# Four seams between layers in a fixed order: sums, norm and columns tile by tile

## The chip, the cores and the metric

The kernel runs on one core of a Trainium2 chip. The metric is the device time of one execution in microseconds (us). The core's engines run side by side, each through its own queue of instructions in order: PE (TensorE, matrix products), DVE (VectorE, elementwise work), ACT (ScalarE, activations and casts), POOL (GpSimd, elementwise work and some transfers) and SP (SyncE), whose queue issues most of the transfers from HBM. Three runs of the kernel before took 2445.11 to 2447.05 us, median 2446.44.

## The reference

Two blocks of two layers each run over 256 tokens of width 1024, in fp32. The first block's layers have a gated delta rule (gdn) and a windowed attention (dsw) as mixers, and a gated feed-forward network (ffn) of hidden size 2816. The second block's layers have an "even" and an "odd" attention over the tokens and a context, and a mixture of 16 experts (MoE). Around each mixer and each ffn or MoE stands the same frame, in which shift, scale and gate come from a conditioning vector through a matrix product (the "ada" work):

```python
def rms_norm(x, gain):
    xf = x.astype(jnp.float32)
    y = xf * lax.rsqrt(jnp.mean(xf * xf, axis=-1, keepdims=True) + RMS_EPS)
    return y * gain.astype(jnp.float32)
...
h_lat = modulate(rmsnorm(x, norm_mix[i]), m[:, :, 0], m[:, :, 1])   # h * (1 + scale) + shift
...
x = x + m[:, :, 2] * y_lat
h_lat = modulate(rmsnorm(x, norm_ffn[i]), m[:, :, 3], m[:, :, 4])
```

So between two layers every token's row of x is finished (x + gate · y), its root mean square is taken, and the scaled, modulated row is what the next matrix product reads. A place where this happens is called a seam here.

## The kernel before

The 256 tokens are two tiles of 128 rows, tile 0 and tile 1. x lies in SBUF with tokens on partitions. A matrix product wants its input with features on partitions, so each tile's 1024 features are turned into 8 blocks ("columns") of 128x128. Products are made in three passes (`mm3`, lines 394 to 398): every fp32 operand is split into a rounded part and the rest, hi and lo for the input, whi and wlo for the weights, and hi·whi, hi·wlo and lo·whi are added up. `split_w` makes whi with a cast on ACT (line 387) and wlo with a subtraction (line 391), which runs on DVE or, for some chunks, on POOL: every sixth in the first ffn, and in the second ffn (`ffn1`) the first four (`pool_next`).

The steps of a seam and their lines are these. The output product of the layer ends in PSUM; per tile and half (512 features) DVE multiplies by the gate (440) and adds to x (442). `norm_rows` squares each half on ACT with a running sum (299), adds the two sums (300), and takes the inverse root with Ln and Exp on ACT (157, 158) and a correction step in 128x1 operations on DVE (156, 159, 161, 162). DVE scales the tile's 1024 features (302). `split_T` transposes 8 blocks on PE (311) into PSUM, modulates them in four steps a chunk of 512, one chunk of a tile on DVE (329) and the other on ACT (326), and casts to hi on ACT (332) and lo on DVE (333). Then the next product's first matmuls can start (396 to 398).

The four seams are: 1, from the output product of gdn to ffn0, near 384 to 395 us; 2, from ffn0 to dsw, near 600 to 615; 3, from dsw to ffn1, near 891 to 906; 4, from ffn1 to the even attention, near 1099 to 1118.

Other work runs beside this chain. The ada products (218) take their weights as they come; the second block's context runs ahead during the first block, with a gather by one-hot products (1720) at seam 3, and its keys for the even attention are split with cast and subtraction (1309, 1310) at seam 4. `gate()` spreads a gate's row over all partitions before the even attention, with two products on POOL (284), four matmuls (288) and two copies on ACT. Line 1598 and 1601 prepare a router's weights.

The order of each engine's instructions is not written by hand: a planner that simulates the timeline places them, and may move any instruction ahead of another as long as data and buffers allow. Two means restrict it: `keep_in_program_order` sets an instruction behind the last one so marked on its engine, and `issue_after` sets it behind a named instruction.

## Time and profile before

| | |
|---|---|
| median of three runs | 2446.44 us (2445.11 to 2447.05) |
| profiled execution | 2443.09 us, its span 2441.3 us |
| mean granted PE clock | 0.941 |
| busy: PE, DVE, ACT, POOL | 87%, 45%, 32%, 13% |
| mean rate of the transfers | 278 GB/s |
| moved in all | 677.57 MB |

The span is what the profiler saw between the first and the last instruction; the time of an execution lies a little above it. Busy shares are averages over stages of different kinds. The first 1290 us are the first block and the even attention, where PE is busy nearly throughout, with short breaks; from then on the experts' weights stream in at up to 427 GB/s, with the odd attention (about 1830 to 1970) between the two mixtures. The granted clock of PE is 1.0 (2.4 GHz) or 0.5 (1.2 GHz) at any moment; a mean over a stretch says how much of each it had.

### The profile page before, as it was taken

The numbers are of one execution on the slowest core, as the hardware profiler recorded it, in microseconds if no ns is written. First come the engines' busy times: TensorE is split into PE (matmuls) and PEld (weight loads), VectorE is DVE, ScalarE is ACT, GpSimd is POOL, SyncE is SP. The second block draws the span as 40 slices with busy tenths as digits, with TensorE's granted clock in tenths as the row PEclk, the third lists the DMA queues.
The fourth block names the chain that finished last, engine by engine and source line by source line (L and its number), as shares of the span: only waits on it lengthen the run. The fifth ranks groups of instructions, "written<-read, shape, count | busy, mean of one in ns | idle before, by whom it ended". The sixth has DMA issues, their size and how long they took to land. (4 is left out here: it accounts for less than half of the span.)

```text
span 2441.3 us, 30277 instructions
## 1 busy us (share of the span) xinstructions
PE 2123.6 (87%) x12053; PEld 1278.1 (52%) x12053; DVE 1100.0 (45%) x2051; ACT 773.9 (32%) x1470; POOL 316.8 (13%) x334
## 2 busy tenths in 40 slices
PE   6987998998999979998988998888888987777777
PEld 3864676786677657885575222222265652222222
DVE  3777357866555575547764121212157731101111
ACT  3564344443555544435443100000047530000000
POOL 3344211112000040003411000000021010000000
PEclk8988998999999979999998999999989989989999
DMA  9657766976332356537746999999921469999998
GB/s 351 247 174 240 238 226 218 362 256 215 126 109 85 126 189 203 167 119 264 296 169 267 425 426 427 425 426 426 415 84 63 162 274 426 426 426 425 427 425 349
DMA packets 152445, 677.57 MB, mean 278 GB/s; under 512 B 15937, under 2 KB 38315, under 8 KB 113648
## 3 DMA queue, kind: packets, MB, share of 16 engines
q1 hardware_dynamic: 143072, 637.98, 67.3%
q0 software_dynamic: 6784, 36.48, 4.3%
q8 instruction: 95, 1.56, 0.3%
q10 hardware_dynamic: 2448, 1.18, 0.2%
q14 instruction: 46, 0.38, 0.0%
HBM read 667.07 MB, written 8.52 MB: 277 GB/s over the span
## 5 line engine op out<-in xcount | busy, mean ns | idle before, releaser
L391 DVE TENSOR_TENSOR wlo<-rawt,whi 128x1024 fp32r<-128x1024 f32 (+2 forms) x257 | 308.7, 1207 | 228.0 <-ACT whi L387 225.6
L387 ACT CAST whi<-rawt 128x1024 fp32r<-128x1024 f32 (+3 forms) x284 | 280.5, 995 | 313.7 <-PE mmt L398 118.9
L1872 PE MATMUL anyt<-rawb,xs 128*32 128x512 f32 x672 | 164.4, 650 | 52.0 <-DMA rawb<-in_w_exp_gate 26.7
L1858 PE MATMUL anyt<-rawb,xs 128*32 128x512 f32 x1472 | 175.2, 614 | 26.6 <-DMA rawb<-in_w_exp_up 17.3
L1832 DVE TENSOR_TENSOR y<-anyt,g 32x512 f32<-32x512 f32 (+1 forms) x120 | 66.4, 553 | 214.7 <-PE anyt L1825 206.9
L1825 PE MATMUL anyt<-rawb,hT 128*32 128x256 f32 (+1 forms) x1056 | 132.9, 491 | 21.2 <-DMA rawb<-in_w_exp_down 11.0
L398 PE MATMUL anyt<-whi,lo 128*128 128x512 f32 (+1 forms) x384 | 144.8, 379 | 1.8 <-DVE lo L333 1.8
L397 PE MATMUL anyt<-wlo,hi 128*128 128x512 f32 (+1 forms) x384 | 145.4, 380 | 1.1 <-DVE wlo L391 1.1
L1877 DVE TENSOR_TENSOR h<-anyt,h 64x512 f32<-64x512 f32 x16 | 11.1, 693 | 281.8 <-ACT h L1876 281.8
L396 PE MATMUL anyt<-whi,hi 128*128 128x512 f32 (+1 forms) x384 | 134.4, 381 | 0.4 <-ACT t L1723 0.4
L1876 ACT ACTIVATE h<-anyt 64x512 f32<-64x512 f32 x16 | 9.4, 589 | 392.4 <-PE anyt L1872 392.4
L1862 ACT ACTIVATE h<-anyt 128x512 f32<-128x512 f32 x16 | 9.6, 597 | 378.1 <-PE anyt L1858 378.1
L1872 PEld LDWEIGHTS anyt<-rawb,xs 128*32 128x32 f32 x672 | 39.3, 118 | 171.0 <-issue 100.7
L1858 PEld LDWEIGHTS anyt<-rawb,xs 128*32 128x32 f32 x1472 | 48.8, 112 | 147.1 <-issue 113.4
L1863 DVE TENSOR_TENSOR h<-anyt,h 128x512 f32<-128x512 f32 x16 | 11.1, 692 | 207.8 <-PE anyt L1858 207.8
L1825 PEld LDWEIGHTS anyt<-rawb,hT 128*32 128x32 f32 (+1 forms) x1056 | 49.5, 128 | 94.3 <-issue 65.0
L218 PE MATMUL adat<-rawt,lhs 128*32 128x512 f32 x448 | 73.6, 665 | 29.0 <-DMA rawt<-in_w_ada 24.9
L391 POOL TENSOR_TENSOR wlo<-rawt,whi 128x1024 fp32r<-128x1024 f32 (+1 forms) x27 | 67.6, 2511 | 237.7 <-ACT whi L387 196.2
L1872 PE MATMUL anyt<-rawt,xs 128*32 128x512 f32 x352 | 78.7, 596 | 10.9 <-DMA rawt<-in_w_exp_gate 7.3
L397 PEld LDWEIGHTS anyt<-wlo,hi 128*128 128x128 f32 x384 | 72.5, 189 | 20.5 <-issue 3.2
L398 PEld LDWEIGHTS anyt<-whi,lo 128*128 128x128 f32 x384 | 72.4, 188 | 16.2 <-DVE lo L333 2.2
L396 PEld LDWEIGHTS anyt<-whi,hi 128*128 128x128 f32 x384 | 71.6, 189 | 16.6 <-issue 0.8
(634 smaller groups left out, 4381.2 us busy)
## 6 DMA issues: line engine op xcount, KB each, us to landing
rawt<-in_w_ada SPq DMA_DIRECT2D x96, 1024.0 KB, 7.0
rawb<-in_w_exp_up SPq DMA_DIRECT2D x41, 2048.0 KB, 27.0
rawb<-in_w_exp_down SPq DMA_DIRECT2D x41, 2048.0 KB, 27.0
rawb<-in_w_exp_gate SPq DMA_DIRECT2D x39, 2048.0 KB, 25.6
rawt<-in_w_exp_gate SPq DMA_DIRECT2D x41, 1024.0 KB, 26.5
rawt<-in_w_ffn_in SPq DMA_DIRECT2D x40, 1024.0 KB, 7.7
rawt<-in_w_exp_up SPq DMA_DIRECT2D x38, 1024.0 KB, 27.0
rawt<-in_w_exp_down SPq DMA_DIRECT2D x31, 1024.0 KB, 27.0
```

Source lines behind the costliest of these rows:

```text
L218: nc.tensor.matmul(bank[32 * j:32 * j + 32, :], lhs[:, k, :], r[:, 0, 512 * j:512 * j + 512], start=(k == 0), stop=(k == 7))
L387: nc.scalar.copy(hi, w)
L391: e.tensor_tensor(out=lo, in0=w, in1=hi.bitcast(F32), op=OP.subtract)
L396: nc.tensor.matmul(ps, xh, wh, start=start, stop=False)
L397: nc.tensor.matmul(ps, xh, wl, start=False, stop=False)
L398: nc.tensor.matmul(ps, xl, wh, start=False, stop=stop)
L1825: nc.tensor.matmul(yb[o:o + M, c:c + n], hT[:, k, :], w[:, i * n:i * n + n], start=(k == 0), stop=(k == KT - 1), **({} if S == 2 else dict ...
L1832: nc.vector.tensor_tensor(out=ys[s][p0:p0 + CAP, 256 * q:256 * (q + n)], in0=yb[o:o + CAP, c:c + 256 * n], in1=g2[o:o + CAP, 256 * q:256 * ...
L1858: nc.tensor.matmul(b[CAP * i:CAP * i + CAP, :], lhs(k0 + j, i % 2), r[:, j, 512 * hf:512 * hf + 512], start=(k0 + j == 0), stop=(k0 + j == ...
L1863: nc.vector.tensor_tensor(out=h, in0=banks[1], in1=h, op=OP.mult)
L1872: nc.tensor.matmul(b[o:o + 32, :], lhs(k0 + j), r[:, j, 512 * hf:512 * hf + 512], start=(k0 + j == 0), stop=(k0 + j == KT - 1), tile_posit ...
L1877: nc.vector.tensor_tensor(out=h[0:64, :], in0=b[64:P, :], in1=h[64:P, :], op=OP.mult)
```

## The change

At the four seams `norm_opens` takes the place of `norm_T`; the context's norm keeps `norm_T`. The squares go into tiles of their own. Instead of scaling the tile and transposing it, DVE scales the identity (`dg`, 128x128) with the inverse roots, and PE multiplies each 128x128 block of x with it, which gives the scaled block transposed. The DVE steps are kept in program order: the modulation's factor A, tile 0's products and sums, tile 0's inverse root and `dg`; at seams 1 to 3 tile 1's last or all products and sums follow only then (`late`). Tile 1's inverse root is set behind tile 0's Exp. The first three splits of the new weights are set behind named steps: the first cast behind tile 0's Exp and its subtraction behind the sums, the next two behind tile 0's last hi and lo. The context's attention, its keys' splits and the router's weights are set behind hi and lo of the norm. `ffn1` gives no split to POOL. `gate()` is called behind the even attention's projections instead of ahead of them, and the first matmuls of the second block's second-layer ada stay in program order. Modulation stays in four steps a chunk.

The diff, without the lines that only pass new arguments or mark one more matmul:

```diff
@@ -153,13 +154,32 @@
-        nc.vector.tensor_scalar(out=v, in0=ss, scalar1=scale, scalar2=eps, op0=OP.mult, op1=OP.add)
-        nc.scalar.activation(out, ss, AF.Ln, scale=scale, bias=self.eps)
-        nc.scalar.activation(out, out, AF.Exp, scale=-0.5)
-        nc.vector.tensor_tensor(out=t, in0=out, in1=out, op=OP.mult)
+        self.keep(nc.vector.tensor_scalar(out=v, in0=ss, scalar1=scale, scalar2=eps, op0=OP.mult, op1=OP.add))
+        self.keep(nc.scalar.activation(out, ss, AF.Ln, scale=scale, bias=self.eps))
+        self.last_exp = self.keep(nc.scalar.activation(out, out, AF.Exp, scale=-0.5))
+        self.keep(nc.vector.tensor_tensor(out=t, in0=out, in1=out, op=OP.mult))
         sg = -1 if neg else 1
-        nc.vector.scalar_tensor_tensor(out=t, in0=t, scalar=-0.5 * sg, in1=v, op0=OP.mult, op1=OP.mult)
-        nc.vector.scalar_tensor_tensor(out=out, in0=t, scalar=1.5 * sg, in1=out, op0=OP.add, op1=OP.mult)
+        self.keep(nc.vector.scalar_tensor_tensor(out=t, in0=t, scalar=-0.5 * sg, in1=v, op0=OP.mult, op1=OP.mult))
+        self.keep(nc.vector.scalar_tensor_tensor(out=out, in0=t, scalar=1.5 * sg, in1=out, op0=OP.add, op1=OP.mult))
+
+    def keep(self, ins):
+        return self.tc.keep_in_program_order(ins) if self.pin else ins
+
+    @contextmanager
+    def pinned(self):
+
+        self.pin = True
+        yield
+        self.pin = False
+
+    @contextmanager
+    def after(self, *names):
+
+        with ExitStack() as es:
+            for n in names:
+                if n in self.behind:
+                    es.enter_context(self.tc.issue_after(self.behind[n].ins))
+            yield
@@ -215,8 +235,10 @@
-                    nc.tensor.matmul(bank[32 * j:32 * j + 32, :], lhs[:, k, :],
-                                     r[:, 0, 512 * j:512 * j + 512], start=(k == 0), stop=(k == 7))
+                    i = nc.tensor.matmul(bank[32 * j:32 * j + 32, :], lhs[:, k, :],
+                                         r[:, 0, 512 * j:512 * j + 512], start=(k == 0), stop=(k == 7))
+                    if held and k == 0:
+                        self.tc.keep_in_program_order(i)
@@ -291,23 +313,32 @@
-    def norm_rows(self, x, t, xn, rsqrt=None):
+    def inv_rms(self, x, t, sq, rsqrt=None):
...
-            nc.scalar.activation(xn[:, 512 * h:512 * h + 512], x[:, t, 512 * h:512 * h + 512], AF.Square, accum_out=s2[:, h:h + 1])
-        nc.vector.tensor_tensor(out=ss, in0=s2[:, 0:1], in1=s2[:, 1:2], op=OP.add)
+            nc.scalar.activation(sq(h), x[:, t, 512 * h:512 * h + 512], AF.Square, accum_out=s2[:, h:h + 1])
+        self.keep(nc.vector.tensor_tensor(out=ss, in0=s2[:, 0:1], in1=s2[:, 1:2], op=OP.add))
         (rsqrt or self.rsqrt_e)(rs, ss, 1, 1.0 / D, 1e-6)
+        return rs
+
+    def norm_rows(self, x, t, xn, rsqrt=None):
+
+        nc = self.nc
+        rs = self.inv_rms(x, t, lambda h: xn[:, 512 * h:512 * h + 512], rsqrt)
...
-    def split_T(self, src, nk, t, hi, lo, A=None, B=None):
+    def split_T(self, src, nk, t, hi, lo, A=None, B=None, diag=None):
...
+                if diag is not None:
+                    nc.tensor.matmul(tp[:, P * j:P * j + P], src[:, P * (k0 + j):P * (k0 + j) + P], diag, start=True, stop=True)
+                    continue
@@ -329,8 +360,8 @@
-                nc.scalar.copy(h, m)
-                nc.vector.tensor_tensor(out=l, in0=m, in1=h.bitcast(F32), op=OP.subtract)
+                ends = nc.scalar.copy(h, m), nc.vector.tensor_tensor(out=l, in0=m, in1=h.bitcast(F32), op=OP.subtract)
+        return ends if A is not None else None
@@ -343,6 +374,36 @@
+    def norm_opens(self, x, gain, sc, sh, hi, lo):
+
+        nc = self.nc
+        late, self.late = self.late, None
+        self.behind, self.nbehind = {}, 0
+        with self.tc.tile_pool(reuse_waits="tile", name="xn", bufs=2, side="right") as pool:
+            def inv(t):
+                rs = self.inv_rms(x, t, lambda h: pool.tile([P, 512], F32, name="xsq"))
+
+                dg = pool.tile([P, P], F32, name="dg")
+                last = self.keep(nc.vector.tensor_scalar(out=dg, in0=self.ident, scalar1=rs, scalar2=None, op0=OP.mult))
+                return dg, last
+
+            A = self.small(KT)
+            with self.pinned():
+                self.keep(nc.vector.scalar_tensor_tensor(out=A, in0=sc, scalar=1.0, in1=gain, op0=OP.add, op1=OP.mult))
+                dg, last = inv(0)
+                exp = self.last_exp
+                if late:
+                    last = late()
+            for t in range(2):
+                if t:
+                    with self.after("exp"):
+                        dg, _ = inv(t)
+                ends = self.split_T(x[:, t, :], KT, t, hi, lo, A, sh, dg)
+                if t == 0:
+                    self.behind = dict(exp=exp, add=last, hi0=ends[0], lo0=ends[1])
+                self.behind.update(hi=ends[0], lo=ends[1])
+                self.nbehind = 3
@@ -384,11 +445,14 @@
-        nc.scalar.copy(hi, w)
+        self.nbehind -= 1
+        with self.after(*("exp",) if self.nbehind == 2 else ("hi0",) if self.nbehind >= 0 else ()):
+            nc.scalar.copy(hi, w)
...
-        e.tensor_tensor(out=lo, in0=w, in1=hi.bitcast(F32), op=OP.subtract)
+        with self.after(*("add",) if self.nbehind == 2 else ("lo0",) if self.nbehind >= 0 else ()):
+            e.tensor_tensor(out=lo, in0=w, in1=hi.bitcast(F32), op=OP.subtract)
@@ -427,7 +491,14 @@
-                if not pairs:
+                if ends and ci == len(cols) - 1:
+                    f = lambda ci=ci, t=t, b=banks[i]: consumer(ci, t, b)
+                    if i == len(tiles) - 1:
+                        self.late = f
+                    else:
+                        with self.pinned():
+                            f()
+                elif not pairs:
@@ -437,16 +508,16 @@
-            nc.vector.tensor_tensor(out=tm, in0=ps, in1=g[:, 512 * ci:512 * ci + 512], op=OP.mult)
+            self.keep(nc.vector.tensor_tensor(out=tm, in0=ps, in1=g[:, 512 * ci:512 * ci + 512], op=OP.mult))
             xs = x[:, t, 512 * ci:512 * ci + 512]
-            nc.vector.tensor_tensor(out=xs, in0=xs, in1=tm, op=OP.add)
+            return self.keep(nc.vector.tensor_tensor(out=xs, in0=xs, in1=tm, op=OP.add))
...
-        self.pool_share, self.pool_next = dict(ffn0=(6, 0), ffn1=(self.NEVER, 4))[key]
+        self.pool_share, self.pool_next = dict(ffn0=(6, 0), ffn1=(self.NEVER, 0))[key]
@@ -501,8 +572,15 @@
-                for h in range(2):
-                    f(h, t, banks[t][h])
+                def sums(t=t):
+                    for h in range(2):
+                        last = f(h, t, banks[t][h])
+                    return last
+                if t and key == "ffn0":
+                    self.late = sums
+                else:
+                    with self.pinned():
+                        sums()
@@ -891,7 +970,7 @@
-                    with self.aside():
+                    with self.aside(), self.after("hi", "lo"):
@@ -1306,8 +1385,9 @@
-                nc.scalar.copy(kh, src)
-                nc.vector.tensor_tensor(out=kl, in0=src, in1=kh.bitcast(F32), op=OP.subtract)
+                with self.after("hi", "lo"):
+                    nc.scalar.copy(kh, src)
+                    nc.vector.tensor_tensor(out=kl, in0=src, in1=kh.bitcast(F32), op=OP.subtract)
@@ -1321,7 +1401,6 @@
-            gate()
@@ -1336,6 +1415,7 @@
+            gate()
@@ -1595,10 +1675,11 @@
-        nc.vector.scalar_tensor_tensor(out=A, in0=sc, scalar=1.0, in1=gain, op0=OP.add, op1=OP.mult)
         wa = rp.tile([P, 2, KT, E], F32, name=f"wa{tag}")
-        for i, m in enumerate((A, sh)):
-            nc.vector.tensor_tensor(out=wa[:, i], in0=w_router, in1=m.unsqueeze(2).to_broadcast([P, KT, E]), op=OP.mult)
+        with self.after("lo"):
+            nc.vector.scalar_tensor_tensor(out=A, in0=sc, scalar=1.0, in1=gain, op0=OP.add, op1=OP.mult)
+            for i, m in enumerate((A, sh)):
+                nc.vector.tensor_tensor(out=wa[:, i], in0=w_router, in1=m.unsqueeze(2).to_broadcast([P, KT, E]), op=OP.mult)
@@ -1958,7 +2039,7 @@
-                        self.norm_T(xc[s], gmix(l), m[:, s, 8:16], m[:, s, 0:8], hi, lo, (0, 1))
+                        self.norm_opens(xc[s], gmix(l), m[:, s, 8:16], m[:, s, 0:8], hi, lo)
@@ -2068,7 +2149,7 @@
-                self.norm_T(x, gmix(l), m[:, 8:16], m[:, 0:8], hi, lo, (0, 1))
+                self.norm_opens(x, gmix(l), m[:, 8:16], m[:, 0:8], hi, lo)
@@ -2079,7 +2160,7 @@
-            self.norm_T(x, gffn(l), m[:, 32:40], m[:, 24:32], hi2, lo2, (0, 1))
+            self.norm_opens(x, gffn(l), m[:, 32:40], m[:, 24:32], hi2, lo2)
```

What the planner makes of it is shown at three places. A name like x<-x,t_5016 reads: written tile, then read tiles.

The first is DVE at seam 2, where ffn0's output becomes x and the norm for dsw begins. Before (the four products L440 stand a few rows above, in a row; modc is the modulation, va the norms' gains, smt small scratch):

```order
L442 TENSOR_TENSOR x<-x,t_5016 128x512
L442 TENSOR_TENSOR x<-x,t_5019 128x512
L442 TENSOR_TENSOR x<-x,t_5040 128x512
L442 TENSOR_TENSOR x<-x,t_5043 128x512
L1601 TENSOR_TENSOR wa_7269<-wr,A_7267 128x128
L338 SCALAR_TENSOR_TENSOR smt<-modc_118,va 128x8
L391 TENSOR_TENSOR wlo<-rawt,whi 128x1024
L300 TENSOR_TENSOR smt<-smt 128x1
L156 TENSOR_SCALAR smt<-smt 128x1
L159 TENSOR_TENSOR smt<-smt 128x1
```

and after, at the same place (the line numbers are those of the changed kernel; gb is the gate; 511 and 513 are 440 and 442, 393 is 338, 322 is 300, 157 is 156, 160 is 159):

```order
L511 TENSOR_TENSOR t_5020<-mmt,gb_120 128x512
L513 TENSOR_TENSOR x<-x,t_5020 128x512
L511 TENSOR_TENSOR t_5023<-mmt,gb_120 128x512
L272 COPY modc_118<-tpt 128x4x4
L393 SCALAR_TENSOR_TENSOR smt<-modc_118,va 128x8
L513 TENSOR_TENSOR x<-x,t_5023 128x512
L322 TENSOR_TENSOR smt<-smt 128x1
L157 TENSOR_SCALAR smt<-smt 128x1
L160 TENSOR_TENSOR smt<-smt 128x1
L162 SCALAR_TENSOR_TENSOR smt<-smt 128x1
L163 SCALAR_TENSOR_TENSOR smt<-smt 128x1
L388 TENSOR_SCALAR dg<-cst,smt 128x128
```

Tile 0's two halves are finished first and its diagonal is made at once; the weight's split and tile 1's products and sums, which stood ahead, now stand behind.

The second is POOL at seam 3, ahead of ffn1 (gr and gt are tables for the even attention). Before:

```order
L1300 TENSOR_SCALAR gr<-gr 128x2x64
L986 COPY gr<-gr 128x8x16 x2
L391 TENSOR_TENSOR wlo<-rawt,whi 128x1024 x3
L1304 TENSOR_TENSOR gt<-gr,ro 128x256 x4
L391 TENSOR_TENSOR wlo<-rawt,whi 128x1024
```

and after:

```order
L1379 TENSOR_SCALAR gr<-gr 128x2x64
L1065 COPY gr<-gr 128x8x16 x2
L1383 TENSOR_TENSOR gt<-gr,ro 128x256 x4
L219 MEMSET brow 128x512
L221 DMA brow<-in_b_ada 4x512
```

The four splits of weights are gone from POOL; they stand on DVE.

The third is PE at seam 4, where ffn1's last matmul (hl) is followed by the even attention's projections (h2i, h2l). Before:

```order
L398 MATMUL mmt<-whi,hl 128x512
L218 MATMUL adat<-rawt,lhs_108 32x512 x8
L288 MATMUL mmt<-t_9138,cst 128x512
L288 MATMUL mmt<-t_9143,cst 128x512
L218 MATMUL adat<-rawt,lhs_108 32x512 x4
L311 MATMUL tpt<-cst,xn 128x128 x8
L218 MATMUL adat<-rawt,lhs_108 32x512 x4
L311 MATMUL tpt<-cst,xn 128x128 x8
L396 MATMUL mmt<-whi,h2i_9148 128x512
```

and after (340 is the product with the diagonal, 238 is 218, 460 to 462 are 396 to 398):

```order
L462 MATMUL mmt<-whi,hl 128x512
L340 MATMUL tpt<-dg,x 128x128 x12
L460 MATMUL mmt<-whi,h2i_9150 128x512
L461 MATMUL mmt<-wlo,h2i_9150 128x512
L462 MATMUL mmt<-whi,h2l_9151 128x512
L460 MATMUL mmt<-whi,h2i_9150 128x512
L461 MATMUL mmt<-wlo,h2i_9150 128x512
L462 MATMUL mmt<-whi,h2l_9151 128x512
L340 MATMUL tpt<-dg,x 128x128 x4
L238 MATMUL adat<-rawt,lhs_108 32x512 x8
L460 MATMUL mmt<-whi,h2i_9150 128x512 x2
```

The columns follow the last matmul directly, tile 1's last four stand among tile 0's projections, and the gate's matmuls and half of the ada matmuls are no longer ahead of the projections (a 32x512 matmul of this list is two records in the trace).

## Rows read from the trace of the kernel before

**Rows 1.** Stretches (us): PE, PEld, DVE, ACT, POOL busy, granted clock, DMA share, GB/s.

```profile
384.00:395.00 11.00, 4.57 (x18) 3.15 (x19) 8.74 (x22) 5.64 (x15) 3.06 (x2) 0.62 0.58 141
...
600.00:615.00 15.00, 7.17 (x24) 4.56 (x24) 11.22 (x32) 8.56 (x24) 6.57 (x12) 0.67 0.97 339
615.00:891.00 276.00, 261.01 (x1257) 194.15 (x1256) 162.81 (x393) 141.22 (x336) 23.43 (x30) 0.95 0.37 122
891.00:906.00 15.00, 8.88 (x29) 6.65 (x28) 10.35 (x22) 9.01 (x20) 9.39 (x6) 0.66 0.16 60
906.00:1099.00 193.00, 190.94 (x888) 155.83 (x888) 97.17 (x100) 84.88 (x101) 5.51 (x8) 1.00 0.52 170
1099.00:1118.00 19.00, 10.23 (x49) 3.62 (x49) 15.57 (x32) 12.40 (x25) 6.09 (x3) 0.82 0.93 338
1118.00:1250.00 132.00, 127.64 (x714) 85.43 (x713) 100.27 (x170) 62.15 (x130) 44.41 (x38) 0.99 0.68 254
1310.00:1830.00 520.00, 451.16 (x2954) 170.66 (x2955) 119.93 (x232) 54.38 (x110) 29.41 (x37) 0.94 0.88 367
```

**Rows 2.** Waits of SP's queue, 1100 to 1320: total us, times, longest.

```profile
SPq L1755 <- DVE wlo L391: 52.2, 2, 46.9
```

**Rows 3.** Order of time, seam 2: start, us, instruction, idle before and releaser.

```profile
599.32 2.48 DVE L440 TENSOR_TENSOR t<-mmt,gb 128x512 f32<-128x512 f32 x4
...
604.72 1.04 ACT L387 CAST whi<-rawt 128x1024 fp32r<-128x1024 f32 x1 [1.21 <-DMA rawt<-in_dsw_w_in]
605.67 0.62 ACT L299 ACTIVATE xn<-x 128x512 f32<-128x512 f32 x1
...
609.13 0.75 DVE L302 TENSOR_SCALAR xn<-x,smt 128x1024 f32<-128x1024 f32 x1
...
610.03 1.94 PE L311 MATMUL tpt<-cst,xn 128*128 128x128 f32 x8 [6.39 <-DVE smt L159]
...
614.67 0.78 PE L396 MATMUL mmt<-whi,hi 128*128 128x512 f32 x1
```

**Rows 4.** The page's costliest groups: the weights' split on DVE, mean in ns.

```profile
L391 DVE TENSOR_TENSOR wlo<-rawt,whi 128x1024 fp32r<-128x1024 f32 (+2 forms) x257 | 308.7, 1207 | 228.0 <-ACT whi L387 225.6
```

**Rows 5.** PE's groups by form: busy us and mean ns of one.

```profile
L784 PE MATMUL anyt<-T,BT 128*128 128x128 f32 x96 | 12.7, 275 | 0.0
```

**Rows 6.** Order of time, seam 3.

```profile
896.61 7.90 POOL L391 TENSOR_TENSOR wlo<-rawt,whi 128x1024 fp32r<-128x1024 f32 x3 [18.29 <-DVE smt L162]
896.62 2.89 DVE L302 TENSOR_SCALAR xn<-x,smt 128x1024 f32<-128x1024 f32 x1
...
906.29 0.50 PE L396 MATMUL anyt<-whi,hi 128*128 128x512 f32 x1 [0.36 <-ACT t L1723]
```

**Rows 7.** Order of time, seam 1.

```profile
384.58 3.44 DVE L442 TENSOR_TENSOR x<-x,t 128x512 f32<-128x512 f32 x2
385.14 2.34 POOL L391 TENSOR_TENSOR wlo<-rawt,whi 128x1024 fp32r<-128x1024 f32 x1 [6.27 <-issue]
...
388.06 0.63 ACT L299 ACTIVATE xn<-x 128x512 f32<-128x512 f32 x1 [2.04 <-DVE x L442]
...
389.82 0.75 DVE L302 TENSOR_SCALAR xn<-x,smt 128x1024 f32<-128x1024 f32 x1
```

**Rows 8.** Order of time, seam 4.

```profile
1097.77 1.29 DVE L440 TENSOR_TENSOR t<-mmt,gb 128x512 f32<-128x512 f32 x2 [4.69 <-PE mmt L398]
...
1103.93 3.36 PE L218 MATMUL adat<-rawt,lhs 128*32 128x512 f32 x16 [4.79 <-DMA rawt<-in_w_ada]
...
1107.22 1.98 PE L288 MATMUL mmt<-t,cst 128*128 128x512 f32 x4
...
1108.59 3.67 DVE L391 TENSOR_TENSOR wlo<-rawt,whi 128x1024 fp32r<-128x1024 f32 x2 [1.97 <-ACT whi L387]
...
1113.35 0.75 DVE L302 TENSOR_SCALAR xn<-x,smt 128x1024 f32<-128x1024 f32 x1
...
1118.44 0.47 PE L396 MATMUL mmt<-whi,h2i 128*128 128x512 f32 x1
```

14 lines of the change are left out of this document (8 added, 6 removed).

## The prediction

> **What bounds the kernel now.** I read the stretches first. TensorE (PE) works nearly without a break between the seams: 190.94 of 193 us from 906 to 1099, 261.01 of 276 from 615 to 891, 127.64 of 132 from 1118 to 1250 [rows 1]. At the four seams it does not: it works 4.57 of 11 us, 7.17 of 15, 8.88 of 15 and 10.23 of 19, with mean granted clocks of 0.62, 0.67, 0.66 and 0.82 [rows 1]. The granted clock is 1.0 or 0.5 (2.4 or 1.2 GHz), so these means are mixtures. The seams hold 6.4 + 7.8 + 6.1 + 8.8 = 29.1 us in which PE stands idle, 1.2% of 2441: the ceiling for a change that only shortens them. From 1310 to 1830 the DMA engines are 0.88 busy at 367 GB/s and carry the experts' weights [rows 1]. Does time won before 1118 survive that? SP's longest wait before that stream is 46.9 us for a weight split of DVE (VectorE) [rows 2]: the stream opens when the attention lets its buffers go, so it starts earlier if the attention ends earlier. I pass gains through in full.
>
> Next I read seam 2 in order of time, as the pattern of all four. The eight instructions that form x + t·g run as four products, then four sums: the products take 599.32 to 601.80, 0.62 each, so tile 0 is not complete before the group of sums. On ACT (ScalarE) a weight cast of 1.04 us stands before a square (604.72, 605.67), and tile 0's scaling starts only at 609.13. Its transposes start at 610.03 after 6.39 us of idle PE and take 1.94 for eight at the low clock; the first projection matmul is at 614.67 [rows 3].
>
> **The change part by part.** The order of work changes, and hardly its amount. Two scalings of 128x1024 at 0.75 [rows 3] leave each seam; two 128x128 products for the diagonals come. Such a product has no row: between nothing and the 0.75 of eight times the columns, I take 0.3. The eight transposes a tile become eight fp32 matmuls of 128x128. A matmul of that shape costs 12.7/96 = 0.13 us at the full clock [rows 5], half of the 1.94/8 = 0.24 that a transpose took at half clock: no difference in price. The pinned rsqrt steps, the later router weights and the context's attention held behind a cast are the same instructions; I cost them at nothing, covered by the solid PE stretches behind each seam, and at 1 to 2 us where that cover is thin.
>
> *Seam 2.* DVE now does tile 0's product, sum, product, sum: 4 x 0.62 from 599.32 and two short operations, so about 602.3. From the last square to the scaling seam 1 shows 389.82 - 388.06 = 1.76 [rows 7]; plus the diagonal's 0.3 the column matmuls start near 604.5 to 605, against 610.03. That is -5.1. Most is given back. Behind the diagonal DVE has tile 1's four operations (2.5) and a split of 1.21 [rows 4] before it may modulate; ACT has tile 1's second square (not before 607.5) before its four modulations (1.5) and two casts. The first projection matmul comes near 612.2, against 614.67: -2.4. Then tile 1's last rsqrt steps stand behind two more splits (2 x 1.21), so its columns come near 616, 3 later than now. PE has tile 0's 24 matmuls to cover this, at 190.94/888 = 0.215 each [rows 1] 5.2 us, so nearly all is hidden. I take -2.0; bounds -5.1 (nothing given back) and +0.6 (tile 1's 3 us paid in full).
>
> *Seam 3.* Now three splits on POOL (GpSimd) run from 896.61 for 7.90, and DVE's scaling of 896.62 beside them takes 2.89 instead of 0.75; projection starts at 906.29 [rows 6]. With no split on POOL this 2.1 us stall goes, and each split costs DVE 1.21. Sixteen gather matmuls that now fill the gap stand ahead of the output projection's end, 16 x 0.215 = 3.4 later. Even so tile 0's columns come near 896.5, and projection near 900.4: -5.9. DVE then has a split before tile 0's modulation and two before tile 1's last parts: 2 x 1.21 given back. I take -3.5; bounds -6 and +1 (the 3.4 of the gather paid and tile 1 late).
>
> *Seam 1.* A POOL split of 2.34 at 385.14 stands beside two sums that take 3.44 instead of 1.24 [rows 7]. Tile 0's columns come some 2.5 sooner. But tile 1's Exp now follows two casts (1.04 each), and its short products run beside the next POOL split. A product of two SBUF inputs beside such a split was held by 2.2 us here, as 3.44 shows, so tile 1 may be held by up to 2.3 again. I take -0.5; bounds -3 and +1.5.
>
> The Trainium skill (GPSIMD Engine Reference, Specifications) says that GpSimd's SBUF interfaces are shared with VectorE and contend with DVE instructions that have two SBUF inputs. Its rule has no lower limit of size, so it speaks against this change: tile 1's 128x1 products fall under it too, at seams 1 and 4 where a POOL split remains. By the rule both are held in full, about 2.3 us each; the two rows above agree for wide operations, and none here shows a 128x1 one.
>
> *Seam 4.* Eight sum operations run from 1097.77, at 0.62 to 0.69 until about 1103; now they are mixed with the context's key splits. The diagonal comes near 1105 and the columns by 1107, against a scaling at 1113.35 that stands behind two splits of 3.67 together [rows 8]. Again most is given back: ACT casts tile 0's first half before it modulates the second, whose low part is ready near 1114.4; steady projection begins near 1115.7, against 1118.44, and 36 matmuls later the lead is about 4. Out of the gap fall 8 of the 32 L218 records at 3.36/16 = 0.21 and the gate's four broadcast matmuls, 1.98 [rows 8]: 1.7 + 2.0 at the low clock, near 2 at the full one, which the solid stretch after it must pay. The gate's two POOL products move behind the projection, where its result is not yet wanted. I take -2.0; bounds -8 (all of the lead kept) and +4 (lead lost to the POOL split, deferred work paid).
>
> *Elsewhere* the planner's order inside the two attentions and of some weight transfers differs. No row prices that: at most the 15 us of idle PE in 615 to 891 [rows 1] can be won, or as much lost; by the nearest row, the solid stretches, I take 0 within 4.
>
> Sum: -0.5 - 2.0 - 3.5 - 2.0 = -8.0. The profiled execution is 2443.1 (span 2441.3), so 2435; its distance to the median 2446.44 I keep, and predict 2438.4.
>
> **The rivals.** (a) *All is given back*: tile 0 comes early, but the seam ends with tile 1 and with the splits, which have not become faster. For it: PE executes in order, and in seam 2 tile 1's columns come 3 us later. Against: tile 0's 24 matmuls cover 5.2. Then only seam 3's stall is won, 2446.4 - 2.1, some 2445 within 4.
> (b) *Tile 1 starves PE*, slower: where tile 1's last low part comes later than 5.2 us behind tile 0's first, PE stops in the middle of the projection and the clock may fall. Paid at all seams by the upper bounds: 1.5 + 0.6 + 1 + 4 = 7.1, so 2453.5. For it: the first splits of the new weights are held behind tile 0's low parts, so weights and tile 1 queue on DVE together. Against: DVE is busy for 0.5 of 906 to 1099 [rows 1].
> (c) *The order by tiles does not take hold*: the operations are pinned only among each other, and other work slips between. The listed order speaks against it; time 2446.
> (d) *A warm PE*: the columns are matmuls, and PE is at full clock sooner. At seam 2 the mean of 0.67 over 15 us means 9.9 us at half clock, about 5 of them with PE working [rows 1, 3]; if the clock rose 2 us sooner, 1 us of work a seam is won: 2434.4.
> The Trainium skill (TensorE: Matmul & The Clock Gate, PE-mode transpose) says that transpose mode does not count as PE-busy for the clock, which is what (d) would follow from. The trace bears it out weakly: the clock was still low after both tiles' transposes of seam 2, but the trace does not tell why.
>
> **How the numbers follow.** Forecast 0.50, (a) 0.22, (b) 0.15, (c) 0.03, (d) 0.10. The range takes (d) and the forecast's own spread (about 6, from the bounds taken as partly independent) below, and half of (b) above: 2428 to 2451. Faster or slower counts beyond 0.2%, 4.9 us, about what can be told here. Faster: 0.80 of the forecast, all of (d), 0.2 of (a): 0.54. Slower: 0.9 of (b) and a little of the others: 0.16. The rest, 0.30, is within.
>
> **What would show it.** Right: in the profile after, seam 2's column matmuls start about 5 us behind the last sum's start of tile 0, at 605, and projection at 612; no POOL split at seam 3 and no DVE operation above 1.5 us there; idle PE over the four seams down from 29 to about 21. Wrong: idle PE between tile 0's and tile 1's matmuls (rival b), first expert transfers that start no earlier although seam 4 ended earlier (passage), or the stretch from 1118 to 1250 longer by more than 3 us (deferred work undervalued).

## The result and the profile after

The changed kernel is slower: 2477.64 us median of four runs (2470.58 to 2482.53) against 2445.78 (2439.29 to 2447.05), a ratio of 1.0125 [1.0105, 1.0146], some 31 us. The forecast was 2438.4 with a range up to 2451. The profiled execution after took 2476.25 us (span 2474.4), that of before 2443.1 (span 2441.3).

The first view is the stretches of the changed kernel, placed so that they answer to those of before [rows 1]. The columns are the same: PE, PEld, DVE, ACT and POOL busy, granted clock, DMA share, GB/s.

```profile
386.00:397.00 11.00, 6.73 (x24) 5.42 (x25) 8.08 (x19) 7.88 (x19) 0.64 (x1) 0.73 0.01 3
404.00:414.00 10.00, 10.00 (x44) 8.05 (x44) 9.63 (x10) 7.21 (x8) 0.63 (x2) 1.00 0.63 206
414.00:440.00 26.00, 26.00 (x112) 18.50 (x110) 25.53 (x23) 9.10 (x11) 3.14 (x2) 1.00 1.02 376
440.00:450.00 10.00, 6.44 (x17) 3.56 (x17) 2.50 (x4) 1.92 (x2) 2.98 (x2) 0.66 1.02 364
610.00:625.00 15.00, 11.93 (x35) 7.76 (x33) 11.48 (x28) 10.14 (x23) 6.69 (x12) 0.60 0.95 292
625.00:922.00 297.00, 267.89 (x1261) 197.66 (x1260) 161.36 (x399) 143.18 (x338) 27.38 (x34) 0.92 0.36 118
922.00:934.00 12.00, 7.59 (x38) 6.33 (x36) 8.38 (x24) 5.29 (x13) 0.00 (x0) 0.85 0.43 132
934.00:1129.00 195.00, 194.03 (x902) 158.29 (x901) 99.37 (x105) 88.11 (x106) 1.87 (x4) 0.99 0.49 160
1129.00:1146.00 17.00, 9.48 (x55) 7.08 (x55) 12.00 (x30) 10.57 (x26) 2.35 (x1) 0.80 0.40 132
1146.00:1282.00 136.00, 126.45 (x742) 86.22 (x743) 102.25 (x175) 65.00 (x133) 48.51 (x40) 1.00 0.72 267
```

PE idles less at the seams than before: 4.3 + 3.1 + 4.4 + 7.5 = 19.3 us in the four windows (55 us in all), against 29.1 in those of before (60 us); the forecast said about 21. Part of this is the columns themselves, which keep PE busy about twice as long as the transposes did (below). Yet the kernel is slower. What grew stands behind two of the seams. The sliding-window stage, 276 us with 15.0 idle and a mean clock of 0.95 before [rows 1], is now 297 us with 29.1 idle at 0.92. The 21 us more are 14.1 of idle time and 6.9 of longer busy time (267.89 against 261.01, for nearly as many matmuls). And in the first feed-forward block there is a hole, 440 to 450, with 6.44 us of work at a mean clock of 0.66. The same three stretches of the kernel before, which the prediction did not look at:

```profile
404.00:414.00 10.00, 9.20 (x40) 7.05 (x39) 10.00 (x9) 5.73 (x7) 0.00 (x0) 1.00 1.02 397
414.00:440.00 26.00, 25.69 (x109) 18.23 (x109) 19.80 (x20) 10.67 (x12) 6.60 (x4) 1.00 0.97 318
440.00:450.00 10.00, 10.00 (x43) 7.19 (x42) 8.44 (x9) 2.00 (x2) 0.03 (x1) 1.00 1.04 403
```

To see where the time went I match each matmul of PE with the same one of before and follow the difference of their starts. Two executions of identical code already differ by several us, so only steps within a stage count, and small ones not even there. In five kernels below whose seam 2 is as before, the difference rises by 0.3 to 3.2 us from 590 to 700: over the 25 us from the seam's start the mean clock is 0.80 in this execution of before, and 0.66 or 0.73 in four of the five. In eight kernels whose seam 4 is as before, it rises by 1.6 to 6.4 us from 1175 to 1290. The steps are +8 between 425 and 460, +17 to +20 between 750 and 910, and the end is at +33. The stream of the experts only passes this on: its second transfer is issued at 1314.73 against 1284.29, and the last at 2458.47 against 2425.08. SP's longest wait ahead of it, for a weight split, is shorter than in [rows 2], yet the stream starts later:

```profile
SPq L1836 <- DVE wlo L455: 42.1, 2, 36.8
```

Seam 2 of the changed kernel in order of time (start, us, instruction, idle before and releaser), which answers to [rows 3]:

```profile
608.65 0.69 DVE L511 TENSOR_TENSOR t<-mmt,gb 128x512 f32<-128x512 f32 x1
...
613.55 0.29 DVE L388 TENSOR_SCALAR dg<-cst,smt 128x128 f32<-128x128 f32 x1
...
613.90 3.79 PE L340 MATMUL tpt<-dg,x 128*128 128x128 f32 x16 [2.40 <-DVE dg L388]
...
621.44 1.98 ACT L450 CAST whi<-rawt 128x1024 fp32r<-128x1024 f32 x2
621.51 0.80 PE L460 MATMUL mmt<-whi,hi 128*128 128x512 f32 x1
...
623.32 0.20 ACT L159 ACTIVATE smt<-smt 128x1 f32<-128x1 f32 x1
...
628.08 1.95 PE L340 MATMUL tpt<-dg,x 128*128 128x128 f32 x16
...
631.37 0.50 PE L460 MATMUL mmt<-whi,hi 128*128 128x512 f32 x1 [1.35 <-ACT hi L363]
```

Counted from the first product, tile 0's columns start after 5.25 us (before 10.71) and the projection after 12.86 (before 15.35). Tile 1's Exp (L159) stands behind two weight casts, and its columns come after 19.4. Behind them PE stops for 1.35 us until tile 1's rows are cast (631.37). The diagonal costs 0.29. A product with the diagonal is two records in the trace and a transpose one: eight products are 16 records, 3.79 us here, where eight transposes took 1.94 [rows 3], both at half clock (1.2 GHz). So the columns took 1.9 us more of PE for tile 0.

Seam 1 and the start of the block behind it:

```profile
387.97 0.69 DVE L511 TENSOR_TENSOR t<-mmt,gb 128x512 f32<-128x512 f32 x1
388.11 3.41 PE L340 MATMUL tpt<-dg,x 128*128 128x128 f32 x16 [2.83 <-DVE dg L388]
...
396.36 2.41 POOL L455 TENSOR_TENSOR wlo<-rawt,whi 128x1024 fp32r<-128x1024 f32 x1 [16.12 <-ACT smt L159]
396.45 2.34 DVE L160 TENSOR_TENSOR smt<-smt 128x1 f32<-128x1 f32 x1
396.56 10.64 SPq L136 DMA_DIRECT2D rawt<-in_w_ada  x2
...
403.73 0.71 POOL L529 COPY smt<-hi 128x1 f32<-128x1 f32 x1 [4.96 <-ACT hi L363]
404.73 0.75 DVE L258 TENSOR_SCALAR adaacc<-rawt,smt 128x1024 f32<-128x1024 f32 x1 [0.33 <-POOL smt L530]
```

The sums of [rows 7] are no longer stretched: each operation takes 0.69 us. In return a 128x1 product of tile 1, 0.16 us elsewhere, takes 2.34 beside the next POOL split. DVE begins the modulation sums (L258: sums of the ada work, which free load buffers) at 404.73; before, these began at 399.03. What they wait for is a copy on POOL that reads tile 1's last cast to hi, so the end of tile 1 decides their start, in both kernels. Counted from the last matmul of the output product, they start after 19.9 us (before 15.5). That copy and SP's load queue in the kernel before:

```profile
383.50 0.37 SPq L135 DMA_DIRECT2D rawt<-in_w_ada  x1
...
398.04 0.70 POOL L458 COPY smt<-hi 128x1 f32<-128x1 f32 x1 [8.53 <-ACT hi L332]
...
401.13 3.01 SPq L135 DMA_DIRECT2D rawt<-in_w_ada  x2
406.26 0.37 SPq L135 DMA_DIRECT2D rawt<-in_w_ffn_in  x1
407.42 0.37 SPq L135 DMA_DIRECT2D rawt<-in_w_ada  x1
```

Before, the loads are issued at 383.5, 401.1, 403.8, 406.3 and 407.4. After, one is issued at 396.56, as a held split ends, and the next only at 406.8. The hole comes 40 us later: PE stops for 3.6 us until a cast is done, and the cast has waited for its transfer:

```profile
442.49 1.04 ACT L450 CAST whi<-rawt 128x1024 fp32r<-128x1024 f32 x1 [4.40 <-DMA rawt<-in_w_ffn_in]
```

Seam 3 answers to [rows 6], seam 4 to [rows 8]:

```profile
928.51 1.16 PE L340 MATMUL tpt<-dg,x 128*128 128x128 f32 x8 [1.83 <-DVE dg L388]
...
932.25 2.07 PE L340 MATMUL tpt<-dg,x 128*128 128x128 f32 x8 [2.58 <-DVE t L360]
...
933.98 0.77 PE L460 MATMUL anyt<-whi,hi 128*128 128x512 f32 x1
...
1134.62 3.75 PE L340 MATMUL tpt<-dg,x 128*128 128x128 f32 x16 [5.97 <-DVE dg L388]
...
1135.75 2.35 POOL L455 TENSOR_TENSOR wlo<-rawt,whi 128x1024 fp32r<-128x1024 f32 x1 [12.52 <-ACT whi L450]
1136.13 1.99 DVE L160 TENSOR_TENSOR smt<-smt 128x1 f32<-128x1 f32 x1 [1.02 <-ACT smt L159]
...
1140.95 0.48 PE L460 MATMUL mmt<-whi,h2i 128*128 128x512 f32 x1
```

At seam 3 no POOL split is left and no DVE operation exceeds 1.4 us. At seam 4 the same short product is held again, 1.99 us. The weights' split on DVE costs what it did [rows 4], 1200 ns in the mean.

For the sliding-window stage, the transfers of the context's attention show when its chain of units ends: its four output pieces go out (L1312, in before L1233), and the whole comes back once for the output product (L1322, in before L1243). A row gives the issues and their first and last start. The kernel before, then after:

```profile
L1233 POOL DMA_DIRECT2D cxo<-t x4: 562/574/590, 657.1 to 796.1; - x4
L1243 SPq DMA_DIRECT2D rawt<-cxo x1: 339/339/339, 798.6 to 798.6; - x1
```

```profile
L1312 POOL DMA_DIRECT2D cxo<-t x4: 557/575/577, 686.4 to 816.0; - x4
L1322 SPq DMA_DIRECT2D rawt<-cxo x1: 339/339/339, 818.5 to 818.5; - x1
```

The first projection matmul of the stage moved by 6.84 us (614.67 to 621.51), the return of the context's output by 19.9: the chain ends 13 us later in the stage. PE's longest waits of the stage after, as us in total, times and longest:

```profile
PE acct L1028 <- DVE pt L1126: 7.2, 4, 6.1
PE tpt L342 <- DMA rawt<-cxo: 5.4, 1, 5.4
```

PE stands at 822.5 for that very return, 5.4 us, and at 886.2 for a copy of the last group's softmax weights on DVE (6.1). Before, no instruction waited for the return.

### The profile page after: what moved, and what is told of

Same layout as the page of the kernel before. It is cut to its first block, busy times and chain, and to the rows that moved or that the text cites. A ratio compares the mean times of both kernels' runs of the same rounds, so it can differ in the third digit from the quotient of the medians.

```text
span 2474.4 us, 30384 instructions
## 1 busy us (share of the span) xinstructions
PE 2136.7 (86%) x12117; PEld 1292.8 (52%) x12117; DVE 1093.2 (44%) x2055; ACT 773.8 (31%) x1470; POOL 305.7 (12%) x330
## 5 line engine op out<-in xcount | busy, mean ns | idle before, releaser
L455 DVE TENSOR_TENSOR wlo<-rawt,whi 128x1024 fp32r<-128x1024 f32 (+3 forms) x261 | 311.6, 1200 | 236.1 <-ACT whi L450 224.7
L1939 PE MATMUL anyt<-rawb,xs 128*32 128x512 f32 x1472 | 175.9, 617 | 27.7 <-DMA rawb<-in_w_exp_up 17.8
L1953 PE MATMUL anyt<-rawb,xs 128*32 128x512 f32 x672 | 158.1, 631 | 44.3 <-DMA rawb<-in_w_exp_up 23.1
L1906 PE MATMUL anyt<-rawb,hT 128*32 128x256 f32 (+1 forms) x1056 | 140.2, 512 | 25.8 <-DMA rawb<-in_w_exp_down 15.6
L238 PE MATMUL adat<-rawt,lhs 128*32 128x512 f32 x448 | 66.8, 655 | 22.0 <-DMA rawt<-in_w_ada 18.0
L460 PE MATMUL mmt<-whi,hi 128*128 128x512 f32 (+1 forms) x192 | 75.5, 410 | 5.7 <-ACT whi L450 4.3
```

The source lines that it names most:

```text
L238: i = nc.tensor.matmul(bank[32 * j:32 * j + 32, :], lhs[:, k, :], r[:, 0, 512 * j:512 * j + 512], start=(k == 0), stop=(k == 7))
L455: e.tensor_tensor(out=lo, in0=w, in1=hi.bitcast(F32), op=OP.subtract)
L460: nc.tensor.matmul(ps, xh, wh, start=start, stop=False)
L1906: nc.tensor.matmul(yb[o:o + M, c:c + n], hT[:, k, :], w[:, i * n:i * n + n], start=(k == 0), stop=(k == KT - 1), **({} if S == 2 else dict ...
L1939: nc.tensor.matmul(b[CAP * i:CAP * i + CAP, :], lhs(k0 + j, i % 2), r[:, j, 512 * hf:512 * hf + 512], start=(k0 + j == 0), stop=(k0 + j == ...
L1953: nc.tensor.matmul(b[o:o + 32, :], lhs(k0 + j), r[:, j, 512 * hf:512 * hf + 512], start=(k0 + j == 0), stop=(k0 + j == KT - 1), tile_posit ...
```

## The experiments

The theory after reading this: the seams did about what was reckoned, and the loss lies behind two of them. (A) At seam 2 the context's attention, held behind the norm, starts its serial chain later, and its tail sticks out at the stage's end. (B) At seam 1 DVE starts the modulation sums late, so buffers and loads come late in a stretch that is full of transfers. The rivals are spelled out in the expectations.

**One seam at a time.** Each of four kernels (e1 to e4 in the expectations) is the kernel before with the change at one seam. In the source, the seams are switched by these lines (here seam 1), and by lines like them for the sums, the holds and POOL's share:

```diff
-            self.norm_T(x, gffn(l), m[:, 32:40], m[:, 24:32], hi2, lo2, (0, 1))
+            if l in (0,):
+                self.norm_opens(x, gffn(l), m[:, 32:40], m[:, 24:32], hi2, lo2)
+            else:
+                self.norm_T(x, gffn(l), m[:, 32:40], m[:, 24:32], hi2, lo2, (0, 1))
```

> Only seam 1 has the new norm (and the bias tables' matmuls in program order, which belong to it); the other three seams are as before. Theory A: what the change costs is not in the seams but in the order that the planner then gives the work behind them; here SP's order of ffn0's weights and the ada weights between 400 and 465. Then the time is about 9 us above before (8 to 11), PE runs dry for about 3.5 us near 440 in wait of a weight cast, and at 410, behind the seam, the work is within 1 us of before. Rival B: the fixed order itself starves PE in the seam (tile 1 late); then the whole loss is there by 410, and ffn0 adds nothing.

> Only seam 2 has the new norm (and the context's attention held behind its casts). Theory A: at 635 the work is within 1 us of before, and the loss comes in the dsw stage between 750 and 890, where the context's attention and output product stand some 20 us later in the order: 12 to 20 us above before, with PE waiting about 5 us for the transfer of the context's attention output. Rival B: the loss is at 610 to 635, in the seam itself, 3 to 10 us, and the dsw stage keeps its length.

> Only seam 3 has the new norm (and no split on POOL in ffn1). Theory A: nearly nothing behind the seam is reordered (6 positions of SP's queue), so the seam's own gain shows: 2 to 6 us below before, with ffn1's first matmul about 3 us earlier. Rival B: tile 1's late columns starve PE here too: 2 to 6 us above.

> Only seam 4 has the new norm (and the gate's spread behind the projections, the ada matmuls in program order). Theory A: the projections start earlier, but the ada weights and matmuls come later and the even attention is reordered; 0 to 4 us above before, with a lead of some 4 us near 1160 that is given back by 1260. Rival B: PE waits 6 us for tile 1's diagonal within the seam, and the whole is 5 to 10 us above, lost before 1140.

Measured: seam 1 2456.92, ratio 1.0044 [1.0028, 1.0060]; seam 2 2467.66, 1.0083 [1.0066, 1.0101]; seam 3 2446.35, 1.0002 [0.9988, 1.0017]; seam 4 2447.40, 1.0007 [0.9992, 1.0022]. The ratios add to 1.36%, the whole change has 1.25%: the loss is seams 1 and 2. In the traces the difference of starts does this: seam 1 about 0 at the seam and +8.3 from 425 to 475; seam 2 about 0 by 650 and a further +17.6 to 890; seam 3 -3.4 at the seam; seam 4 a lead of 4.0 by 1175 (6.3 to 2.3), which is given back by 1250 (8.4). So theory A came true at seams 1, 2 and 4 in time and place. Two things did not. At seam 3 the time does not show the 2 to 6 us. And at seam 2 PE waited only 1.4 us for the return of the context's output, not 5: that wait is a sign that the chain is late, and little of the price. The hole of seam 1 is in its own kernel too:

```profile
440.00:450.00 10.00, 5.66 (x15) 3.00 (x15) 2.48 (x4) 1.46 (x2) 2.99 (x2) 0.66 1.03 372
```

**Seam 2, with the hold taken off, and the hold alone.** The first is the kernel of seam 2 with this edit, the second the kernel before with the reverse edit (and its norm made to hand out its last cast and low part):

```diff
-                    with self.aside(), self.after("hi", "lo"):
+                    with self.aside():
```

> Seam 2 alone has the new norm, as in e2, but the context's attention is not held behind the norm's last cast and subtraction. Theory A1: the hold makes the context's attention start late and, being a chain of units that wait for each other, stay late through dsw; freed, most of the 20 us of e2 goes: 0 to 8 us above before. In the order its second to sixth units still stand later than before by 40, 40, 55, 4 and 7 matmuls and its last by 68, so some loss in the stage's tail may stay. Rival A2: the fixed sums and columns themselves displace it; then 15 to 20 us stay.

> The kernel before, all four seams with the old norm; only the context's attention is held behind the old norm's last cast and subtraction at seam 2. The context's matmuls stand at the same places among the others as in e2. Theory A1: the hold alone makes the loss, 14 to 20 us above before, all of it between 640 and 890. Rival A2: within 4 us of before.

Measured: the hold alone 2469.39, 1.0103 [1.0077, 1.0130]; seam 2 without it 2457.58, 1.0043 [1.0026, 1.0059]. So the hold by itself, with nothing of the seam changed, costs as much as the whole of seam 2. Its seam is as before (the starts lie at +1.8 at 640), and the chain ends late all the same. The time is a little above the 14 to 20 us of theory A1:

```profile
L1314 POOL DMA_DIRECT2D cxo<-t x4: 557/574/577, 676.6 to 810.7; - x4
L1324 SPq DMA_DIRECT2D rawt<-cxo x1: 339/339/339, 813.2 to 813.2; - x1
```

That is 14.6 later than before. PE waits only 0.9 us for it. Its longest waits in the stage are for the softmax of the last groups and for tiles behind it; that the context's work had covered these is argued, not shown:

```profile
PE acct L1030 <- DVE pt L1128: 3.9, 3, 3.0
PE tpt L342 <- DVE oTl L348: 2.8, 1, 2.8
```

But without the hold +11 us stay, which lies between the two theories. PE's order shows why. I count in the traces the matmul records of other work between the stage's first projection and each of the 24 value products of the context's attention. In the kernels with seam 1, 3 or 4 alone the count is that of before throughout. In the whole change, in seam 2 alone and in the hold alone the products come 0 to 73 records later, half of them 48 or more; in seam 2 without the hold still 0 to 80, half of them 34 or more. So the hold acts through the order that the planner then writes.

**Seam 1: splits not held, and one more buffer.** The first leaves the first casts and splits of the new weights where the planner wants them, the second gives the block a sixth extra buffer for raw weights. Both are edits of the kernel of seam 1, shown with the rest of their lines cut:

```diff
-                self.nbehind = 3
+                self.nbehind = 0
...
-self.more_raw(5, key=key):
+self.more_raw(6 if key == "ffn0" else 5, key=key):
```

> Seam 1 alone, as in e1, but the first three splits of ffn0's weights are not held behind tile 0's steps. Theory A3: in e1 tile 1's short steps stand behind the held splits and beside a split on POOL (one product took 2.34 us), so DVE comes 5.7 us later (404.7 instead of 399.0) to the ada sums that let the weight buffers go, SP's next load is issued at 406.8 instead of 401.1, and the stretch from 402 to 450, in which the DMA engines are busy throughout, starves PE near 440. With the splits free DVE is back at the ada sums by about 400 and the loss of 9 falls to 0 to 4. Rival A4: SP's changed order of ada and ffn loads makes the loss by itself; that order stays changed here, and 7 to 10 us stay.

> Seam 1 alone, as in e1, with a sixth extra weight buffer in ffn0. Theory A3: one load of 1 MB more is on its way before the buffers come free, worth about 3 us of the DMA engines' time (1 MB at 350 GB/s): 3 to 7 us above before instead of 9, with a shorter hole near 440. Rival A4: an order at fault is not mended by a buffer: 7 to 11 above.

Measured: free splits 2452.19, 1.0022 [1.0007, 1.0038]; the buffer 2472.21, 1.0117 [1.0086, 1.0147]. The free splits settle little. The time is 5.6 us above before, between the theories, and its interval overlaps that of seam 1; in the trace the loss from 385 to 500 is 7.8, against 8.3 with the holds. What the edit was meant to do did not happen. Counted from the last matmul of the output product, the modulation sums start after 18.6 us, with the holds 18.7, before 15.5. Only the load of 396.5 goes out earlier, at 384.21. So this run leaves open whether the late sums or the order of the loads make the hole.

The buffer run fits neither theory and says nothing sure on seam 1: with another supply of buffers the planner chose another order for the sliding-window stage too, within 6 records that of the run without the hold, and lost 16 us there, although seam 2 is that of before. It was no part of the question, but it shows that this order of the context's units costs that much without any diagonal columns.

**The fixed order with the old columns.** This kernel has the fixed order by tiles at seam 2, but scales the rows and transposes them as before, and does not hold the context's attention. In its trace the context's value products stand where they stood before, but for one unit that comes 16 records earlier. Seam 3 is as changed. A second kernel has seam 4 as well. The core of the edit to the changed kernel:

```diff
+                if turn:
+                    dg = pool.tile([P, D], F32, name="xn")
+                    last = self.keep(nc.vector.tensor_scalar(out=dg, in0=x[:, t, :], scalar1=rs, scalar2=None, op0=OP.mult))
+                    return dg, last
...
-                    with self.aside(), self.after("hi", "lo"):
+                    with self.aside():
```

> Seam 2 in the fixed order by tiles, but with the old steps on the data (scaled rows and transposes in place of the diagonal columns) and with the context's attention not held; seam 3 as changed; seams 1 and 4 as before. In this kernel TensorE takes the context's attention in the sliding-window stage at the places it had before (within 3 matmuls). Theory (the loss at seam 2 is the order of the context's attention in the stage behind, not the seam's own order): the stage 650 to 890 costs nothing, seam 3 gives its 3.4 us, seam 2 between 0 and -2: 1 to 5 us under before, ratio 0.998 to 1.000. Rival (the fixed order at seam 2 itself delays what follows, through vector work put behind it): 8 us or more over before.

> As the run before it, with seam 4 in the fixed order too (its sums, its gate rows later, its key splits behind the norm). Theory (seam 4's lead is given back before the stage ends, as in the run of seam 4 alone): within 2 us of the kernel without it. Rival (the lead lasts where the stage before is on time): 3 us or more under it, 5 to 8 under before.

Measured: 2447.42, 0.9998 [0.9986, 1.0010], and with seam 4 2449.50, 1.0006 [0.9992, 1.0019]. The stage's loss is gone:

```profile
L1317 POOL DMA_DIRECT2D cxo<-t x4: 564/574/590, 666.0 to 802.8; - x4
L1327 SPq DMA_DIRECT2D rawt<-cxo x1: 339/339/339, 805.3 to 805.3; - x1
```

This execution already stood 6.7 us behind that of before at 700, so the chain ends at the same place of the stage (805.3 - 6.7 = 798.6). The starts lie at +6.7 at 700 and +7.0 at 875. Seam 3 then takes 2.4 us off (+4.7 at 950). At seam 2 itself the difference grows by 2.6 (+4.1 at 575, +6.7 at 700), no more than in executions whose seam 2 is as before (0.3 to 3.2), so a cost of the old columns in the fixed order is not shown. The rival, 8 us or more, is excluded; the 1 to 5 us under before did not show either. So there is no version here that beats the kernel before. Seam 4 again leads by 4 at 1175 (9.5 to 5.4) and is 3.2 behind by 1250.

The pins are in this kernel as in seam 2 without the hold, and the diagonal columns are not; seam 3 stands behind the stage. So it is the columns as matmuls that bring the planner to the later order when nothing is held.

**Vector time at seam 1, by itself.** The kernel before, with five more copies of one 0.75 us product at the place of the modulation sums:

```diff
                        elif k + j == 0:
+                            first, self.first = self.first, False
+                            for _ in range(6 if first else 1):
                                 nc.vector.tensor_scalar(out=acc, in0=r[:, 0, :], scalar1=w1, scalar2=None, op0=OP.mult)
```

> Kernel before, with nothing changed at any seam but that the first product of the first modulation sum behind seam 1 is done six times on the vector engine (five more of 0.75 us, 3.75 us of vector time at 399 us; the same values are written again). Theory (vector time lost at seam 1 is not made up in the stretch to 450 us, where the vector engine and the transfers are full, so the first four weights of the stretch and the buffers come late and TensorE runs dry near 440): 4 to 8 us over before, the loss between 425 and 460 us. Rival (the stretch has room for it, and seam 1's loss comes from the order of its transfers or of its held casts alone): 1.5 us over before or less.

Measured: 2453.49, 1.0023 [1.0010, 1.0036], 6.1 us by the medians; in the trace +4.7 between 425 and 460. Two windows of it:

```profile
400.00:410.00 10.00, 10.00 (x40) 7.84 (x38) 9.45 (x15) 5.09 (x9) 0.89 (x2) 0.90 0.11 12
...
450.00:460.00 10.00, 7.37 (x28) 4.70 (x27) 9.29 (x11) 4.37 (x6) 0.00 (x0) 0.83 1.04 405
```

This execution is already 4.4 us behind ahead of the edit. Its first load behind the seam is issued at 409.52, so 4.0 later than before at the same place in the work. The DMA engines nearly rest (0.11), are then full, and 40 us later PE runs dry. At the same place of the kernel before, they have 0.44:

```profile
395.60:405.60 10.00, 9.85 (x40) 7.58 (x38) 9.52 (x13) 5.37 (x8) 0.89 (x2) 0.93 0.44 123
```

3.75 us of DVE time at this place came back as a loss of 4.7 us in the trace and of 6.1 by the medians (interval 2.4 to 8.8). In this kernel the order of a few loads changed as well, as it did at seam 1. So what is shown is that a late DVE, with the order of loads that the planner then writes, is enough; the two are not told apart.

**The whole change without the hold.**

> The whole change, with the context's attention not held behind the seam 2 norm. Theory (the pieces add: seam 1 +9, seam 2 without the hold between 0 and +11, seam 3 -3.4, seam 4 and the even stage 0 to +3): the hold's share goes, 2452 to 2468, that is 10 to 25 us under the whole change. Rival (the hold isn't what costs in the whole change): 2472 or more.

Measured: 2465.36, 1.0066 [1.0050, 1.0083]: about 14 us of the 31 go (1.25% less 0.66%), somewhat more than the 0.40% between the two kernels of seam 2. The hold is the largest single part of the loss, and the pieces add up.

The kernels side by side. The second column is how many records later half of the context's value products come, or more. The third is how much later its output returns, the last what is lost by 950; both are less what the execution was behind ahead of seam 2. In the rows with a star seam 3 is changed too, and its gain lies in the last column.

| kernel | order later by | return later, us | lost by 950, us |
|---|---|---|---|
| the hold alone | 48 | 12.7 | 22.6 |
| seam 2 | 48 | 11.2 | 18.1 |
| the whole change * | 48 | 9.5 | 19.1 |
| one more buffer | 36 | 14.3 | 17.7 |
| seam 2 without the hold | 34 | 10.5 | 15.7 |
| the whole change without the hold * | 10 | 16.4 | 10.6 |
| old columns, seams 2 and 3 * | 0 | 2.6 | 0.6 |
| old columns, seams 2 to 4 * | 0 | 5.5 | 3.3 |

A late order and a late end of the chain go with a loss in every row, and neither is there without it. The size of the loss follows the order; it does not follow the time of the return, which is latest where 10.6 are lost.

## Why the prediction was wrong, point by point

*What bounds the kernel, and the passage to the end:* right. The second transfer of the experts moved by 30.4 us, the end by 33. The sign I had not foreseen passed through in the same way.

*Seam 2, the term of -2.0:* its steps came as worked out, and whether its sum did can't be told. Columns 5.25 us behind the first product (reckoned 5.2 to 5.7), projection after 12.86 (reckoned 12.9). Tile 1's columns came at 19.4, reckoned 16.7, because its Exp waits for two casts on ACT. PE stopped 1.35 us for tile 1, and the lead of 2.5 was used up: the kernel of seam 2 stands at +0.4 by 650, near the upper bound, +0.6. But executions with an untouched seam 2 stand at +0.3 to +3.2 there. One price was misread: "no difference in price" between a transpose and an fp32 product divided 12.7 us by 96 records, and a product is two of them. At half clock eight products took 3.79 us, eight transposes 1.94. This is 1.9 us a tile that the sum has at nothing.

*Seam 3, -3.5:* right, -3.4 in its own kernel's trace. Of this its time shows -1.4 by the medians, and the interval [-2.9, +4.2] allows little more.

*Seam 1, -0.5:* right for the seam, where the forecast tile 1 held beside POOL came true. The Trainium skill (GPSIMD Engine Reference, Specifications) has GpSimd contend with two-input DVE instructions; the rows agree down to a 128x1 product, 2.34 and 1.99 us instead of 0.16. What I left out is the work that waits for tile 1's end, the modulation sums, which free the load buffers. They started 5.7 us later (some 4 beyond the 1.4 by which this execution was behind at 380), and the stretch behind, where the transfers have a share of 1.02 and DVE 25.53 of 26 us, could not make it up: 3.6 us of PE idle for a cast and a low clock behind it, +8 us. That the late sums do this, and not the changed order of the loads that came with them, is argued. I had counted such stretches as "the solid PE stretches behind each seam" that cover; this one did not cover.

*Seam 4, -2.0:* the lead of 4 came and was gone by 1250, so +1.7 [-2.0, +5.4]. From 1175 to 1290 the four kernels with seam 4 changed lose 8.3 to 9.4 us against before, and the eight with the old one 1.6 to 6.4. So 2 us or more belong to the change; that it is the work moved behind the seam is argued, not shown. Within the bounds, mis-sized by about 4.

*"I cost them at nothing" and "Elsewhere ... 0 within 4":* this is the step that failed, with some 17 to 20 of the 31 us. The context's attention held behind a cast is indeed the same instructions, but they form a serial chain woven into the stage. With the hold, half of its value products come 48 or more records later and its output returns 13 us later; the stage's idle PE rose from 15.0 to 29.1 us and its busy time, at a mean clock of 0.92 instead of 0.95, from 261.0 to 267.9. The hold alone costs 1.03%. The reckoning named a bound, "at most the 15 us of idle PE ... or as much lost", which the loss exceeds, and then took the nearest row, a solid stretch. That row says that PE is full; it doesn't say that the side chain has slack.

*The rivals:* (b) came nearest in time, mostly by another mechanism. Its sign is there: PE stops for 1.35 us between the tiles' projections at seam 2 (631.37). But this is 1.35 of 31 us, and the loss lies behind the seam. (d) is not borne out: over the 25 us from the start of seam 2 the mean clock is 0.73 with columns as matmuls, and 0.66 to 0.80 where the seam is untouched. (c) falls with the rows of seam 2, which stand in the fixed order.

*Open:* why the planner answers the hold, the diagonal columns or one more buffer with a later order was not traced, nor how a later order turns into each single wait; that the order costs 11 to 16 us without the hold is shown by the kernel with one more buffer and, from the other side, by the old columns. At seam 1 the late sums and the order of the loads are not told apart.

## What to carry to other kernels

When an edit holds back a side chain, ask where its units then stand and where the chain ends, not what it costs: a serial chain woven into a full engine is not free because the engine is busy. And when an engine's work ends late, follow what it releases: if that is the buffers of a stretch whose transfers are full, the delay can come back as idle PE, with the half clock on top. A change in one place can make a planner order a stage anew 200 us further on, so the order of each stage behind it has to be compared, and its side chains with it. A seam of 15 us can't be judged by one execution of each kernel: here the clock alone moved an untouched one by up to 3 us.

## What the hardware showed that I had not expected

A 128x1 product on DVE, 0.16 us by itself, took 2.34 and 1.99 us beside a POOL split. Both times it ended as the split ended (398.79 behind 398.77, 1138.12 behind 1138.10), so the hold is the POOL operation's remaining time and not a share of the DVE operation's. An fp32 product of 128x128 is two records in the trace and took twice a transpose of that size (3.79 against 1.94 us for eight, both at half clock). And idle PE was not the whole price of idle PE: in the hole of seam 1, 3.6 us of waiting came with a mean clock of 0.66 over ten us, and the loss was 8.
